# One large product a step ahead of the scores, the values of a pair in two runs, and norm rows on VectorE

## The chip, the core and the metric

The kernel runs on one core of a Trainium2 chip. The metric is the device time of one execution in microseconds (us). Engines are named as in the profile: PE is TensorE, DVE VectorE, ACT ScalarE, POOL GpSimd, SP SyncE, which issues the DMAs. Each engine takes its own instructions strictly one after the other, so an instruction that waits holds up everything behind it on its engine.

## The reference

One layer of a diffusion backbone with 128 context tokens and 1024 latent tokens, that is nine blocks of 128 tokens (block 0 is the context), of width 1024. Two head groups, attention and a bidirectional mLSTM, read one input projection and share one output projection, and a SwiGLU FFN follows. Cut to the part that the change touches:

```python
q = rope(rmsnorm(h @ w_q, q_norm_w))                  # 8 query heads of 64, 2 key/value heads
s = einsum('bqhgd,bkhd->bhgqk', q, k) * scale         # latent block: 128 rows x 1152 keys (1024 latent + 128 cached)
o = einsum('bhgqk,bkhd->bqhgd', softmax(s), v)
x = x + g1 * (concat([o, hm], -1) @ w_out)            # hm: the mLSTM heads; w_out has an hm half and an attention half
h2 = rmsnorm(x, norm2_w) * (1 + sc2) + sh2
x = x + g2 * swiglu(h2, w_gu, w_down)
```

Operands are split in a high and a low part (`hi`, `lo`), and three products stand for one, which keeps float32 accuracy.

## The kernel before

The program is written in three parts: projections and the mLSTM scan, then attention, then the FFN. The change is in the second. It is a loop over 64 heads (8 latent blocks of 8 query heads), one head a step, with an order that is written by hand (`manual_schedule`): each engine's instructions stand in the order in which the Python code emits them.

**What a step does for the softmax** (`step(n)`, L1490). PE makes the scores of head n+2 (`head_scores`, six matmuls into the PSUM tile `S`, L1110). `S` has five banks; even and odd heads lie at its two ends and share the middle bank. DVE forms the reciprocal of head n's sum (L1506), then the maximum of head n+1 (`head_max`, L1114), then the low part of head n's probabilities (`pl`, L1517). ACT makes the high part of head n (`ph`, L1509) and the exponential of head n+1 (`head_exp`, L1118). SP turns `ph` and `pl` by DMA. The scores of head n+2 take the place of head n's, so they wait for the exponential of head n. The maximum of head n+1 stands behind the scores of head n+2 in the program and reads the bank that they share with it.

**The values.** Two heads make a pair, and in each odd step PE multiplies the turned probabilities of an earlier pair with the values (`value_products`, L1053, 18 matmuls into `po`). ACT and POOL add up the result one step later (`value_sums`, L1058 to L1061).

**The fillers.** All other work of this part is cut into tasks (generators), and a planner (`Filler`, L1232) puts their pieces into the steps: the second half of the query projection (`q_task`), its rope, which runs on POOL, the turning of the queries (`turn_task`), the hm half of the output projection (`hm_task`), its attention half with the second norm (`mix_task`), and the splitting of `w_out` (`w_task`). Each piece names its engine, a cost and the least number of steps since the piece before it. Each engine has a credit a step, and a piece is taken while the credit is above zero and the piece's condition holds. `fl.run("PE")` emits the PE pieces; the ACT and DVE pieces of a step are emitted at its end, behind that step's `ph`, exponential and `pl`. A large piece on PE is half of a block's query projection or one `out_block` (L1138): 12 matmuls of 512 columns. Two PSUM banks serve all fillers. A product's bank is free again when DVE has read it (`add_gated`, L1133, which makes a tile `t` that POOL adds to `x`), a turned block's when DVE has made its low part (`ring`, `qT`).

**Rows of the second norm.** `norm_rows` (L1428) scales a block's 1024 columns by its reciprocal root mean square, in two ACT instructions of 512 columns (L1432); PE turns them, ACT and DVE apply the modulation.

## Time and profile before

| what | us |
|---|---|
| median of 3 runs (lowest, highest) | 1640.9 (1636.6, 1645.5) |
| the profiled execution's own time | 1645.3 |
| its span, first to last instruction | 1643.5 |
| PE, DVE, ACT, POOL busy | 1489.5, 902.0, 732.4, 251.1 |
| first maximum of the loop's filler steps to the last one (455.88 to 799.94 in the span) | 344.1 |
| from there to the first FFN product (837.45) | 37.5 |

The profiled execution is 4.4 us above the median. The page gives busy time and the costliest groups of instructions for the whole span; for the loop, the views over stretches and the instructions in order of time say more, since engines wait for each other there in every step.

### The profile page before, as it was taken

How to read it: one execution, taken by the hardware profiler on the slowest of the kernel's cores; microseconds unless marked ns; L12 is line 12 of the kernel's file. 1: busy time of each engine (PE TensorE's matmuls, PEld its weight loads, DVE VectorE, ACT ScalarE, POOL GpSimd, SP SyncE). 2: the span in 40 equal slices, each digit the busy share in tenths (PEclk: the TensorE clock that was granted, in tenths of full speed). 3: DMA queues.
4: the chain of work that ended last, by engine and by line, in shares of the span. 5: the costliest groups of instructions: out<-in, count | busy, mean ns of one | idle time of the engine just before them, and what ended most of it. 6: DMA issues, size and time to landing. Idle time of an engine off the chain costs nothing.

```text
span 1643.5 us, 22904 instructions
## 1 busy us (share of the span) xinstructions
PE 1489.5 (91%) x8651; PEld 921.1 (56%) x8651; DVE 902.0 (55%) x2160; ACT 732.4 (45%) x1428; POOL 251.1 (15%) x272
## 2 busy tenths in 40 slices
PE   5899999898596799877689989999999999999995
PEld 2755666575454677655455555456664466655542
DVE  3844355849765777877645456333353333442278
ACT  3744343345465666778655666003340032422023
POOL 0411021303224522333320000000000000000001
PEclk8899999999598899999799999999999999999998
DMA  9345462301285789556357553421104310120213
GB/s 353 114 142 150 93 144 62 73 1 19 60 174 99 149 190 193 101 102 127 72 180 252 184 194 100 140 93 52 52 27 141 115 52 28 50 77 14 83 59 116
DMA packets 281685, 181.83 MB, mean 111 GB/s; under 512 B 167302, under 2 KB 253782, under 8 KB 281574
## 3 DMA queue, kind: packets, MB, share of 16 engines
q1 hardware_dynamic: 280150, 177.96, 41.6%
q10 hardware_dynamic: 1424, 2.40, 0.4%
q8 instruction: 68, 1.11, 0.3%
q14 instruction: 43, 0.35, 0.1%
HBM read 122.71 MB, written 19.29 MB: 86 GB/s over the span
## 4 chain that ended last, share of the span: by engine, by line
PE 37%; DMA 5%; DVE 4%; ACT 4%; issue 1%; POOL 0%; ACTq 0%; SPq 0%; DVEq 0%; POOLq 0%
PE mm L1180 8%; PE mm L1182 8%; PE mm L1181 8%; PE mm L1751 4%; PE mm L1752 4%; PE mm L1753 4%; DMA wd_d<-wdt 3%; DMA wdt<-in_w_down_dram 2%; DVE x L1136 1%; ACT wdt L1546 1%; DVE wdt L1552 1%; ACT wdt L1551 1%; DVE t L1135 1%; ACT jk L1576 0%; ACT jk L1837 0%
## 5 line engine op out<-in xcount | busy, mean ns | idle before, releaser
L1180 PE MATMUL mm<-h,wpair 128*128 128x384 f16 x1056 | 345.0, 327 | 1.5 <-DVE fl L1453 1.5
L1181 PE MATMUL mm<-h,wpair 128*128 128x384 f16 x1056 | 345.0, 327 | 0.0
L1182 PE MATMUL mm<-h,wpair 128*128 128x384 f16 x1056 | 344.7, 327 | 0.0
L1714 DVE SCALAR_TENSOR_TENSOR tn<-tn,mm 128x384 f32<-128x384 f32 x66 | 36.4, 552 | 217.5 <-PE mm L1182 139.6
L1751 PE MATMUL mm<-wd,hl 128*128 128x512 f16 x396 | 149.9, 379 | 0.0
L1752 PE MATMUL mm<-wd,hl 128*128 128x512 f16 x396 | 149.9, 379 | 0.0
L1753 PE MATMUL mm<-wd,hl 128*128 128x512 f16 x396 | 149.6, 379 | 0.0
L1180 PEld LDWEIGHTS <-wpair 128*128 128x128 f16 x1056 | 105.4, 100 | 67.3 <-issue 0.7
L1182 PEld LDWEIGHTS <-wpair 128*128 128x128 f16 x1056 | 103.5, 98 | 68.7 <-issue 0.7
L1181 PEld LDWEIGHTS <-wpair 128*128 128x128 f16 x1056 | 103.5, 98 | 68.7 <-issue 2.3
L1110 PE MATMUL S<-kst,qT 128*128 128x512 f32 (+1 forms) x384 | 97.3, 394 | 47.9 <-ACT pr L1118 46.0
L499 PE MATMUL wi<-ipair,hT 128*128 128x384 f16 (+2 forms) x384 | 124.7, 325 | 2.8 <-ACT ipair L216 2.8
L1840 POOL TENSOR_TENSOR x<-x,fw 128x512 f32<-128x512 f32 x9 | 11.5, 1274 | 756.7 <-ACT jk L1837 756.7
L501 PE MATMUL wi<-ipair,hT 128*128 128x384 f16 (+2 forms) x384 | 124.4, 325 | 0.4 <-POOL hT L135 0.4
L500 PE MATMUL wi<-ipair,hT 128*128 128x384 f16 (+2 forms) x384 | 124.7, 325 | 0.0
L1717 ACT ACTIVATE jk<-tn 128x384 bf16<-128x384 f32 x66 | 34.4, 521 | 196.8 <-DVE tn L1715 145.1
L1576 ACT ACTIVATE jk<-braw 128x1024 bf16<-128x1024 f32 x44 | 45.9, 1044 | 152.9 <-DVE x L1136 152.1
L1517 DVE SCALAR_TENSOR_TENSOR pl<-pr,st,ph 128x1152 f16<-128x1152 f32 x64 | 95.1, 1486 | 31.9 <-ACT ph L1509 29.0
L1509 ACT ACTIVATE ph<-pr,st 128x1152 f16<-128x1152 f32 x64 | 80.3, 1254 | 68.0 <-issue 59.6
L1110 PEld LDWEIGHTS S<-kst,qT 128*128 128x128 f32 x384 | 69.9, 208 | 72.2 <-ACT pr L1118 58.6
L1114 DVE TENSOR_REDUCE st<-S 128x1 f32<-128x1152 f32 x64 | 86.7, 1355 | 39.9 <-PE S L1110 39.4
L1135 DVE SCALAR_TENSOR_TENSOR t<-mm,gm,gl 128x512 f32<-128x512 f32 x64 | 47.7, 745 | 81.3 <-PE mm L1753 81.3
(427 smaller groups left out, 2854.5 us busy)
## 6 DMA issues: line engine op xcount, KB each, us to landing
wd<-wd_d SPq DMA_DIRECT2D x58, 512.0 KB
braw<-in_w_gu_dram SPq DMA_DIRECT2D x44, 512.0 KB
a4s<-in_w_ada_dram SPq DMA_DIRECT2D x32, 512.0 KB
wdt<-in_w_down_dram SPq DMA_DIRECT2D x22, 512.0 KB
wd_d<-wdt SPq DMA_DIRECT2D x22, 512.0 KB
aw<-in_w_ada_dram SPq DMA_DIRECT2D x16, 512.0 KB
x<-in_x_sample_dram SPq DMA_DIRECT2D x16, 512.0 KB
iraw<-in_w_in_dram SPq DMA_DIRECT2D x32, 256.0 KB
```

The lines of the kernel that those rows point to most:

```text
L499: mm(ps[:, :n], ah, wh[:, k % 2, c0 : c0 + n], start=(k == 0), stop=False)
L500: mm(ps[:, :n], ah, wl[:, k % 2, c0 : c0 + n], start=False, stop=False)
L501: mm(ps[:, :n], al, wh[:, k % 2, c0 : c0 + n], start=False, stop=(k == KD - 1))
L1110: mm(S[:, lo:hi], qTs[b][:, h, :], kst[kv][:, t, lo:hi], start=(t == 0), stop=(t == 1))
L1114: dve.tensor_reduce(out=stat[n][:, 0:1], in_=score[n], axis=AX.X, op=ALU.max, negate=True)
L1180: mm(ps, wh[:, k, :], th[:, k, :], start=(k == 0), stop=False)
L1181: mm(ps, wh[:, k, :], tl[:, k, :], start=False, stop=False)
L1182: mm(ps, wl[:, k, :], th[:, k, :], start=False, stop=(k == KD - 1))
L1517: dve.scalar_tensor_tensor(out=pl, in0=pr, scalar=st[:, 3:4], in1=ph, op0=ALU.mult, op1=ALU.subtract)
L1751: mm(ps, ah, w[:, k, 0], start=(j + k == 0), stop=False)
L1752: mm(ps, ah, w[:, k, 1], start=False, stop=False)
L1753: mm(ps, al, w[:, k, 0], start=False, stop=(j + k == g["nf"] - 1))
```

## The change

- Within a step the order on PE is now: the second part of a pair's values (even steps), the fillers, the scores of head n+2, the first part of a pair's values (odd steps). Before, the scores came first, then the fillers, then a whole pair's values.
- The 18 value matmuls of a pair are issued as 10 at the end of an odd step and 8 at the start of the next; their sums are emitted in the step of the second part.
- The planner takes at most one PE piece of a cost over 2.0 in a step, and the credit of PE is 3.3 a step, before 3.5.
- The rope of a pair of query blocks starts no earlier than three steps after the previous pair's rope was emitted; before, it only had to be emitted.
- `norm_rows` is one DVE instruction of 1024 columns in place of two ACT instructions of 512, for the nine blocks, with one buffer; `norm2`, which does the last block, calls it too.
- The loop runs for at least one more step.

```diff
@@ -1042,12 +1042,13 @@
             return q_rest[:, b - CB].rearrange("p (k g) d -> p k (g d)", g=2)
         return ap2.tile([P, 4, P], F32, name=nm("oT"), tag="oT", bufs=3)
 
-    def value_products(b, j, nk, kv, rhs):
-        if j == 0:
+    def value_products(b, j, nk, kv, rhs, po=None, part=(0, NB)):
+        if j == 0 and po is None:
             oT[b] = new_oT(b)
-        po = po2[:, n_po[0] % 2 * 256 : n_po[0] % 2 * 256 + 256]
-        n_po[0] += 1
-        for n in range(nk):
+        if po is None:
+            po = po2[:, n_po[0] % 2 * 256 : n_po[0] % 2 * 256 + 256]
+            n_po[0] += 1
+        for n in range(nk)[slice(*part)]:
             v = vs[:, NB if nk == 1 else n, kv].rearrange("p t d -> p (t d)")
             for t in range(2):
                 mm(po, v, rhs(t, n), start=(n == 0 and t == 0), stop=(n == nk - 1 and t == 1))
@@ -1151,11 +1152,9 @@
         both = new() if new else fp.tile([P, KD, P], F32, name=nm("fl"), tag="fl", bufs=1)
         cnd = 0 if b == 0 else 1
         pss = []
-        for half in range(2):
-            y = fp.tile([P, 512], F32, name=nm("y"), tag="y", bufs=2)
-            act(y, x1[b][:, half * 512 : (half + 1) * 512], AF.Copy, scale=rs[b])
-            pss.append(y)
-            yield 0.1
+        pss += norm_rows(b)
+        yield 0.1
+        yield 0.1
         for half, y in enumerate(pss):
             ps = bank()
             for j in range(4):
@@ -1233,7 +1232,7 @@
 
         def __init__(self, **per_step):
             self.per_step, self.credit = per_step, dict.fromkeys(per_step, 0.0)
-            self.tasks, self.step, self.banks = [], 0, 2
+            self.tasks, self.step, self.banks, self.big = [], 0, 2, -1
 
         def add(self, gen):
             self.tasks.append([gen, None, self.step - 1])
@@ -1252,6 +1251,10 @@
                         break
                     if not behind and self.credit.get(engine, 1.0) <= 0.0 or ready is not None and not ready():
                         break
+                    if engine == "PE" and cost > 2.0:
+                        if self.big == self.step:
+                            break
+                        self.big = self.step
                     if engine in self.credit:
                         self.credit[engine] -= cost
                     self.banks -= need
@@ -1265,7 +1268,7 @@
         def free(self, n=1):
             self.banks += n
 
-    fl = Filler(PE=3.5, ACT=1.9, DVE=2.0)
+    fl = Filler(PE=3.3, ACT=1.9, DVE=2.0)
     at = {}
 
     def stamp(name):
@@ -1293,7 +1296,7 @@
         fl.free()
         if rope is None:
             return
-        yield "ACT", 1.1, 0, 0, lambda: b - 2 < CB or ("rope", b - 2) in at
+        yield "ACT", 1.1, 0, 0, lambda: b - 2 < CB or since(("rope", b - 2), 3)
         next(rope)
         yield "DVE", 1.1
         next(rope)
@@ -1398,7 +1401,7 @@
         rs[b] = rsqrt1(w, 1.0 / D)
         if b == NB - 1:
             return
-        yield "ACT", 1.35, 1, 0, lambda: b == 0 or ("turned", b - 1) in at
+        yield "DVE", 0.75, 1, 0, lambda: b == 0 or ("turned", b - 1) in at
         ys = norm_rows(b)
         yield "PE", 1.5, 1, 2
         pss = norm_turn(ys)
@@ -1426,12 +1429,9 @@
         return w
 
     def norm_rows(b):
-        ys = []
-        for half in range(2):
-            y = fp.tile([P, 512], F32, name=nm("y"), tag="y", bufs=2)
-            act(y, x1[b][:, half * 512 : (half + 1) * 512], AF.Copy, scale=rs[b])
-            ys.append(y)
-        return ys
+        y = fp.tile([P, D], F32, name=nm("y"), tag="y", bufs=1)
+        dve.tensor_scalar(out=y, in0=x1[b], scalar1=rs[b], scalar2=None, op0=ALU.mult)
+        return [y[:, 0:512], y[:, 512:1024]]
 
     def norm_turn(ys):
         pss = []
@@ -1491,16 +1491,20 @@
         b, h = heads[n] if n < len(heads) else (NB, 0)
         fl.step = n
         fl.begin()
-        if n + 2 < len(heads):
-            head_scores(n + 2)
-        fl.run("PE")
         now = []
         if n < 2:
             now = [value_products(*first_values[2 * n + i]) for i in range(2)]
-        elif n % 2 == 1 and (n - 3) // 2 in pairs:
+        elif n % 2 == 0 and half:
+            args, po = half.pop()
+            now = [value_products(*args, po, (5, NB))]
+        fl.run("PE")
+        if n + 2 < len(heads):
+            head_scores(n + 2)
+        if n % 2 == 1 and (n - 3) // 2 in pairs:
             m = (n - 3) // 2
             two = pairs.pop(m)
-            now = [value_products(heads[2 * m][0], m % 4, NB, m % 4 // 2, lambda t, i: two[t][:, :, i, :])]
+            args = (heads[2 * m][0], m % 4, NB, m % 4 // 2, lambda t, i: two[t][:, :, i, :])
+            half.append((args, value_products(*args, None, (0, 5))[2]))
         if n < len(heads):
             st, pr = stat.pop(n), prob.pop(n)
             dve.reciprocal(st[:, 2:3], st[:, 1:2])
@@ -1516,13 +1520,8 @@
                 head_exp(n + 1)
             dve.scalar_tensor_tensor(out=pl, in0=pr, scalar=st[:, 3:4], in1=ph, op0=ALU.mult, op1=ALU.subtract)
             dma_t(two_n[1][:, h % 2, :, :], pl)
-        for v in late:
+        for v in now:
             value_sums(*v)
-        late[:] = now
-        if n < 2:
-            for v in late:
-                value_sums(*v)
-            late[:] = []
         fl.run("X")
         for behind in (False, True):
             for e in ("ACT", "DVE"):
@@ -1606,7 +1605,7 @@
             dve.tensor_scalar(out=v[:, 7:8], in0=v[:, 4:5], scalar1=v[:, 5:6], scalar2=wds[:, self.f, 3:4], op0=ALU.mult, op1=ALU.mult)
 
 
-    pairs, late = {}, []
+    pairs, half = {}, []
     pieces = [Piece(0, lambda: wp.tile([P, 1024], F32, name=nm("braw"), tag="raw", bufs=2), ("whi", "wlo"))]
     pieces += [Piece(f) for f in range(1, NF)]
     with tc.manual_schedule(engines=ENGINES):
@@ -1632,7 +1631,7 @@
         head_max(0)
         head_exp(0)
         n = 0
-        while n < len(heads) + 4 or fl.tasks:
+        while n < len(heads) + 5 or fl.tasks:
             step(n)
             if n >= len(heads):
                 fl.credit = dict.fromkeys(fl.credit, 5.0)
```

How this moves instructions on PE, around the hm half of the output projection (`mm<-wlo,ring` is such a product, `S` the scores, `ident` marks a turning, and `[waits ...]` names the engines whose counters the instruction waits for). Before, between the scores of heads 29 and 31:

```order
L1110 MATMUL S_4796<-kst_4271,qT_5807 128x512 x4
L1142 MATMUL mm_6250<-wlo_5012,ring_5704 128x512 [waits DVE_49,PE_49]
...
L1144 MATMUL mm_6250<-wlo_5015,ring_5704 128x512
L1110 MATMUL S_4796<-kst_4271,qT_5807 128x512 [waits Activation_49]
L1110 MATMUL S_4796<-kst_4271,qT_5807 128x512 x3
L1110 MATMUL S_4796<-kst_4271,qT_5807 128x128 x2
```

And now, between the same scores:

```order
L1143 MATMUL mm_6219<-wlo_5199,ring_5761 128x512 [waits DVE_49]
...
L1111 MATMUL S_4796<-kst_4271,qT_5798 128x128 [waits Activation_49]
L1111 MATMUL S_4796<-kst_4271,qT_5798 128x128
L1111 MATMUL S_4796<-kst_4271,qT_5798 128x512 x4
L114 MATMUL mm_6260<-ident,t_1157_6120 128x128 [waits DMAHW7_49,DVE_49]
L114 MATMUL mm_6260<-ident,t_1157_6120 128x128 x3
L1143 MATMUL mm_6265<-wlo_4999,ring_5762 128x512 [waits DVE_49]
...
L1111 MATMUL S_4796<-kst_4271,qT_5798 128x512 [waits Activation_49]
```

In both lists scores and large products take turns. What moved is the product's step: before, the product that stands behind the scores of head 30 was emitted in step 28; now it is emitted in step 29, ahead of the scores of head 31. The DVE counter that it waits for is that of the row `t_1182` below, in step 28 on DVE, which reads the bank of the product before it (`mm_6219`):

```order
L1115 TENSOR_REDUCE st_6246<-S_4796 128x1 [waits PE_49]
L1521 SCALAR_TENSOR_TENSOR pl_6241<-pr_6201,st_6199,ph_6240 128x1152 [waits DMAHW2_49,Activation_49]
L1134 TENSOR_TENSOR t_1182_6257<-mm_6219,gl_4866 128x512 [waits Pool_49]
L1510 RECIPROCAL st_6246<-st_6246 128x1 [waits Activation_49]
```

The first of these rows is the maximum of head 29, and the PE counter that it waits for is reached by the scores of head 30, as before the change. So the row that frees the bank now stands on DVE behind a maximum that needs the scores just ahead of the product.

The second place is the first turning of query block 3 on PE, which reads what the rope on POOL has written (`q_rest`). Before, and then now:

```order
L1110 MATMUL S_4796<-kst_4270,qT_4856 128x512 [waits Activation_49]
L1110 MATMUL S_4796<-kst_4270,qT_4856 128x512 x3
L1110 MATMUL S_4796<-kst_4270,qT_4856 128x128 x2
L114 MATMUL mm_5342<-ident,q_rest 128x128 [waits DVE_49,PE_49,Pool_49]
L114 MATMUL mm_5342<-ident,q_rest 128x128 x3
L1287 MATMUL mm_5301<-ipair_4262,hT_293 128x512
```

```order
L1111 MATMUL S_4796<-kst_4270,qT_4856 128x512 x4
L114 MATMUL mm_5306<-ident,q_rest 128x128 [waits PE_49,Activation_49,Pool_49]
L114 MATMUL mm_5306<-ident,q_rest 128x128 x3
L1290 MATMUL mm_5268<-ipair_4262,hT_293 128x512
...
L1111 MATMUL S_4796<-kst_4270,qT_4856 128x512 [waits Activation_49]
```

The turning is in step 9 in both. Before, it stood behind the scores of head 11; now those scores stand behind it. The rope that it waits for was emitted in step 6 before and is emitted in step 7 now.

## The prediction

> **What bounds the kernel now.** I read the view by stretches first, cut at the maxima of heads 3, 21, 44 and 63 and at the first FFN product (columns: us, then busy us of PE, its weight loads, DVE, ACT and POOL, each with its instructions, PE's granted clock, DMA share, GB/s).
>
> ```profile
> 455.88:566.10 110.22, 86.33 (x448) 57.96 (x447) 74.49 (x124) 67.72 (x93) 49.02 (x44) 0.89 0.67 128
> 566.10:684.25 118.15, 108.99 (x601) 86.45 (x600) 95.29 (x137) 81.18 (x112) 36.26 (x44) 1.00 0.86 175
> 684.25:799.94 115.69, 88.29 (x471) 66.99 (x472) 88.27 (x172) 88.33 (x141) 43.55 (x46) 0.95 0.57 107
> 799.94:837.45 37.51, 24.65 (x105) 18.00 (x104) 14.97 (x42) 17.96 (x32) 13.59 (x15) 0.80 0.48 130
> 837.45:1643.50 806.05, 780.40 (x4418) 432.97 (x4417) 356.00 (x852) 270.04 (x517) 16.66 (x13) 0.99 0.31 98
> ```
>
> The FFN holds half of the span with PE busy for 97% of it, and no edit reaches into it but one norm. In the loop (the first three rows, 60 steps in 344 us, 5.7 us a step) PE is busy for 78, 92 and 76%, and no engine is full: what sets the step is who waits for whom. The view of waits over the same 344 us (in total, times, longest):
>
> ```profile
> PEld S L1110 <- ACT pr L1118: 53.6, 33, 8.8
> PE S L1110 <- ACT pr L1118: 41.6, 25, 8.3
> DVE st L1114 <- PE S L1110: 35.2, 32, 3.2
> ACT pr L1118 <- DVE st L1114: 22.6, 21, 3.2
> ```
>
> That is a ring: scores wait for an exponential, a maximum for scores, an exponential for a maximum. The instructions in order of time show one turn of it (start, us, engine; heads 29 to 31):
>
> ```profile
> 604.42 1.42 PE L1110 MATMUL S<-kst,qT 128*128 128x128 f32 x6 [0.86 <-ACT pr L1118]
> 606.05 0.47 PE L1142 MATMUL mm<-wlo,ring 128*128 128x512 f32 x1 [0.21 <-DVE qT L135]
> 606.32 1.36 DVE L1114 TENSOR_REDUCE st<-S 128x1 f32<-128x1152 f32 x1
> 606.36 0.40 PE L1143 MATMUL mm<-wlo,ring 128*128 128x512 f32 x1
> 606.59 0.40 PE L1144 MATMUL mm<-wlo,ring 128*128 128x512 f32 x1
> 607.66 1.42 DVE L1517 SCALAR_TENSOR_TENSOR pl<-pr,st,ph 128x1152 f16<-128x1152 f32 x1
> 607.72 1.23 ACT L1118 ACTIVATE pr<-S,st 128x1152 f32<-128x1152 f32 x1
> 609.00 0.68 DVE L135 TENSOR_TENSOR ring<-mm,ring 128x512 fp32r<-128x512 f32 x1
> 609.08 1.37 PE L1110 MATMUL S<-kst,qT 128*128 128x512 f32 x6
> 609.60 0.68 DVE L1133 TENSOR_TENSOR t<-mm,gl 128x512 f32<-128x512 f32 x1
> 610.48 1.36 DVE L1114 TENSOR_REDUCE st<-S 128x1 f32<-128x1152 f32 x1
> 616.67 0.27 PE L1053 MATMUL po<-phT,vs 128*128 128x256 f16 x1
> 616.78 0.27 PE L1053 MATMUL po<-plT,vs 128*128 128x256 f16 x1
> 617.68 1.40 PE L1110 MATMUL S<-kst,qT 128*128 128x128 f32 x6
> 619.12 1.36 DVE L1114 TENSOR_REDUCE st<-S 128x1 f32<-128x1152 f32 x1 [2.12 <-PE S L1110]
> ```
>
> From the maximum at 606.32 to the next at 610.48 are 4.16 us: maximum, exponential (607.72), scores (609.08). The last two rows show that a maximum ends its wait with the scores just made, which are those of the head after its own. Beside this ring, at no cost, PE makes a large product (606.05 to the scores at 609.08: 3.03 us) and DVE makes `pl` and reads the bank of a product (609.60).
>
> **The change part by part.** *Fillers ahead of the scores.* Between the scores of two heads there is one large product before and after. The lists of instructions show what differs: the product there now belongs to the later step, and its first matmul waits for the DVE row at the end of the step before it, mostly for one of the two PSUM banks, since a turned block holds the other. That row stands on DVE behind a maximum, and this maximum behind the scores that have just left PE. The ring becomes longer: scores, maximum, `pl`, the bank's reading, product, scores. By the rows above: maximum to `pl` 1.34 (606.32 to 607.66), `pl` to the next row 1.34 (to 609.00), reading 0.68, product 3.03, scores to the next maximum 1.40 (609.08 to 610.48), in all 7.8 us where the short ring needs 4.2. Other rows that come first on DVE, ACT or POOL are added, from these groups (busy us, mean ns) and from the first and last row of a reciprocal root on DVE:
>
> ```profile
> L1133 DVE TENSOR_TENSOR t<-mm,gl 128x512 f32<-128x512 f32 x32 | 21.9, 686 | 17.9 <-PE mm L1144 17.8
> L135 DVE TENSOR_TENSOR qT<-mm,qT 64x512 fp32r<-64x512 f32 x12 | 8.3, 689 | 0.3
> L135 DVE TENSOR_TENSOR wlo<-raw,wlo 128x1024 fp32r<-128x1024 f32 x4 | 4.7, 1219 | 0.0
> L135 POOL TENSOR_TENSOR kst<-oT,kst 128x512 fp32r<-128x512 f32 x5 | 6.4, 1277 | 4.3 <-ACT kst L1419 4.1
> L1432 ACT ACTIVATE y<-x,r 128x512 f32<-128x512 f32 x16 | 10.6, 710 | 2.3 <-DVE r L1196 2.3
> L340 DVE TENSOR_SCALAR x<-x,ry 128x1024 f32<-128x1024 f32 x9 | 6.4, 750 | 0.0
> ...
> 802.73 0.15 DVE L1189 TENSOR_SCALAR r<-r 128x1 f32<-128x1 f32 x1
> 804.78 0.21 DVE L1196 TENSOR_SCALAR r<-r 128x1 f32<-128x1 f32 x1
> ```
>
> I went through the new list step by step and noted for each PE piece whether its wait ends in the step just before. For the stretch of heads 21 to 44 (23 steps): 17 such products, 17 x 7.8 = 132.6; rows ahead of the one waited for, 7.6 (a second 0.7 us evacuation in three steps, `w_out` splits of 1.22 and query halves of 1.4 in three more); two steps in which only transpositions wait, 12.2; four steps by the short ring or by PE alone (value run 2.0, which is 18 matmuls 0.11 apart, product 3.0, scores 1.4), 19.4. Sum 171.8 for 118.2: **+53.6**. Heads 44 to 63 (19 steps): 9 x 7.8 = 70.2; 15.0 for what comes first (POOL's 1.28 for a mix block, in five steps, the reciprocal root of about 2.2 in two, and a modulation that waits for POOL in one); five transposition steps 36.3 (6.7 to 9.1 each); five others 27.0. Sum 148.5 for 115.7: **+32.8**. Heads 3 to 21 (18 steps): four serial steps 33.1, thirteen of 4.3 to 6.6 together 70.1, and the rope's step, below, 17.4. Sum 120.6 for 110.2: **+10.4**. If a product's 12 matmuls cost their spacing alone (0.23 from 606.36 to 606.59, 2.76) and nothing is lost in between, a serial step is 7.2 and the 30 of them give 18 back; that is the lower bound of the unit price.
>
> *The rope.* Before, ACT waits 7.83 us for POOL:
>
> ```profile
> 486.10 1.90 POOL L669 TENSOR_TENSOR q_rest<-q_rest,ry 128x1024 f32<-128x1024 f32 x1 [1.00 <-POOL oT L1061]
> 495.36 2.34 POOL L687 TENSOR_TENSOR q_rest<-q_rest,nr 128x1024 f32<-128x1024 f32 x1
> 497.73 1.06 ACT L663 ACTIVATE nr<-q_rest 128x1024 f32<-128x1024 f32 x1 [7.83 <-POOL q_rest L687]
> 501.18 2.39 PE L1110 MATMUL S<-kst,qT 128*128 128x512 f32 x6 [8.26 <-ACT pr L1118]
> ```
>
> The new condition removes this wait. But the rope takes POOL 11.6 us (486.10 to 497.70) and is now emitted a step later, and the turning that reads it stands ahead of the scores of head 11. So PE is held until POOL is done: 11.4 from the step's maximum, then turning 0.9, half a projection 3.7, scores 1.4, which is the 17.4 above. The stall goes from ACT to PE and grows by a few us.
>
> *One large product a step.* Before, the five steps with two products stretch their step and the next (heads 29 to 31 to 8.6 between scores, 609.08 to 617.68). This goes; the sums above hold it.
>
> *Norm rows.* Per block, 2 x 0.71 leave ACT and, by the nearest row (L340, same shape), 0.75 comes to DVE. ACT is at most the second longest in the new steps, so I count no gain; at most it is 9 x 1.42 = 12.8. In three steps the row stands ahead of a bank's reading and is in their 6.7; were all nine exposed, 6.8.
>
> *Values in two runs.* Nothing stands between the two parts on PE, and their sums keep their place: 0. If an emission gap opened between them, it would fall into PE's idle time.
>
> *The end.* One product and one transposition move behind the last head, the last pair's values come earlier: of 37.5 us I take 2 off (bounds 4 off, 5 on).
>
> *PE's clock.* The longer ring leaves PE idle for about 3.3 us in each serial step without values. What idling does, the trace shows:
>
> ```profile
> 548.50:552.00 3.50, 3.23 (x11) 2.84 (x12) 1.40 (x4) 2.82 (x6) 3.42 (x3) 0.51 0.62 117
> 548.77 2.40 PE L1110 MATMUL S<-kst,qT 128*128 128x512 f32 x6 [2.79 <-ACT pr L1118]
> 815.61 0.80 PE L1142 MATMUL mm<-wlo,kst 128*128 128x512 f32 x1 [4.67 <-DVE fl L1453]
> 820.47 0.63 PE L1144 MATMUL mm<-whi,kst 128*128 128x512 f32 x1
> ```
>
> After 2.79 idle the scores take 2.40 in place of 1.40 at a granted 0.51; after 4.67 a product takes 5.3 (815.61 to its last at 820.47, and 0.43 more), 2.3 above 3.03. About 16 gaps of 3.2 us and more are new: none cold is 0, all cold 16 x 2.4 = 38. I take 10: the price of the shorter gap, 1.0, for ten of them, since 3.3 us is nearer to 2.79 than to 4.67 and not every gap need go cold. The Trainium skill (TensorE: Matmul & The Clock Gate, "Part 1: The HAM clock gate") says that the clock halves after an idle window of about 3.4 us; by this rule only the six or so longest gaps would count, an estimate of 6 x 1.7 = 10. Here the trace differs: 2.79 us was enough at 548.77.
>
> Sum: 10.4 + 53.6 + 32.8 - 2 + 10 = 105. Against the profiled execution, 1645.3 + 105 = 1750; that execution lies 4.4 above the median, so **1746** for the median.
>
> **The rivals.** (1) *The products fill the wait for the exponential.* If the DVE rows they wait for are done when PE comes to them, the order is a gain: the rope's 7.8, and about 8 for three double steps (12.8 for two steps, where two average ones take 10.4). 1640.9 - 16 = 1625. For it: PE idles 41.6 us ahead of scores. Against it: the wait in the list points at a row of the step before, behind the maximum, 3.4 us after the scores end, not before them. It decides if fewer than about four steps are serial, at 3.6 each. (2) *Bank waits do not bind.* If a product meets a free bank, some 19 of 26 products in the last two stretches wait for nothing late, at 2.5 each (7.8 less 5.3, the mean of 4.2 and 6.4): 1746 - 48 = 1698. For it: there are two banks and one product a step. Against it: a turned block holds one of them for two steps. (3) *A cold PE.* All 16 gaps cold: 28 more than I took, 1774. For it: both gaps quoted above went cold, the shorter one at 2.79 us.
>
> **How the numbers follow.** The forecast has a chance of 0.56, a cold PE 0.22, unbinding banks 0.14; the last 0.08 is (1) and what lies between it and no change: 0.05 for a gain, 0.03 for none. About 8.2 us, 0.5%, is what a measurement tells from no change. So slower 0.92, same 0.03, faster 0.05. The range goes from (2) less 8, for a unit price nearer 7.2, to (3) with 11 for the end and the norm rows: 1690 to 1785. It leaves (1) out.
>
> **What would show it.** Right: large products (L1143 to L1145) of the loop wait for DVE `t`, `ring` or `fl`, some 60 us in all, where scores wait for ACT `pr` now; maxima 7.5 to 8 us apart for heads 29 to 33, where PE is about two thirds busy; one turning that waits some 10 us for POOL `q_rest`, and no such wait of ACT L663; the FFN unchanged at about 806. Wrong: maxima 4 to 6 us apart there, or scores that still wait for `pr`. Half clock in one stretch of the loop would speak for (3).

## The result, and the profile after

The changed kernel takes 1787.6 us (median of four runs, 1787.2 to 1793.4), the kernel before, measured beside it on the same chip, 1643.2: a ratio of 1.089, interval 1.085 to 1.094. The forecast was 1746 with a range from 1690 to 1785. Direction and place were right, and the time lies 2.6 us above the range.

The view by stretches of the changed kernel, cut at the same heads as in the prediction and with the first three heads ahead of them, and that first stretch of the kernel before (us, then busy us of PE, its weight loads, DVE, ACT and POOL, PE's granted clock, DMA share, GB/s):

```profile
440.30:465.59 25.29, 13.79 (x51) 7.49 (x51) 8.81 (x12) 10.19 (x15) 2.25 (x5) 0.73 0.42 100
465.59:590.45 124.86, 89.69 (x430) 57.83 (x428) 76.02 (x123) 66.89 (x91) 44.01 (x39) 0.84 0.55 107
590.45:776.55 186.10, 128.37 (x594) 100.97 (x595) 90.37 (x126) 80.13 (x110) 37.88 (x45) 0.87 0.53 114
776.55:939.08 162.53, 112.13 (x474) 84.51 (x473) 89.61 (x185) 81.73 (x130) 43.78 (x48) 0.74 0.42 78
939.08:981.02 41.94, 25.34 (x114) 18.79 (x113) 21.10 (x48) 17.96 (x31) 17.78 (x17) 0.86 0.42 113
981.02:1791.60 810.58, 785.77 (x4418) 434.89 (x4417) 356.86 (x853) 268.66 (x515) 16.66 (x13) 0.98 0.31 97
```
```profile
439.86:455.88 16.02, 11.51 (x39) 6.61 (x40) 8.82 (x13) 10.09 (x15) 1.84 (x5) 0.68 0.70 163
```

Of the 148.1 us between the two profiled executions, 129.4 lie in the loop from head 3 to head 63 (+14.6, +68.0, +46.8), 9.3 in the first three heads, 4.4 between head 63 and the FFN, 4.5 in the FFN and 0.4 ahead of it all. PE has more busy time in the stretch of heads 21 to 44 (128.4 us for 109.0) with seven matmuls fewer in its records: its clock fell from 1.00 to 0.87.

The view of waits over heads 3 to 63 of the changed kernel (us in total, times, longest):

```profile
DVE st L1115 <- PE S L1111: 208.2, 52, 12.9
ACT pr L1119 <- DVE st L1115: 185.2, 49, 12.6
...
PE mm L1143 <- DVE t L1134: 29.6, 11, 5.5
...
PE S L1111 <- ACT pr L1119: 17.8, 13, 2.8
```

Before, scores waited 41.6 us for the exponential and the maximum 35.2 for the scores. Now the maximum waits 208 us for scores, and what these stand behind is a product that waits for a row of DVE. Two turns of the ring, heads 30 to 32, in order of time (start, us; rows of the ring alone):

```profile
665.85 1.36 DVE L1115 TENSOR_REDUCE st<-S 128x1 f32<-128x1152 f32 x1 [3.95 <-PE S L1111]
667.13 1.41 DVE L1521 SCALAR_TENSOR_TENSOR pl<-pr,st,ph 128x1152 f16<-128x1152 f32 x1
668.45 0.69 DVE L1134 TENSOR_TENSOR t<-mm,gl 128x512 f32<-128x512 f32 x1
669.19 0.51 PE L1143 MATMUL mm<-wlo,ring 128*128 128x512 f32 x1 [1.40 <-DVE t L1134]
672.09 1.32 PE L1111 MATMUL S<-kst,qT 128*128 128x128 f32 x6
673.44 1.36 DVE L1115 TENSOR_REDUCE st<-S 128x1 f32<-128x1152 f32 x1 [4.05 <-PE S L1111]
676.04 0.68 DVE L135 TENSOR_TENSOR ring<-mm,ring 128x512 fp32r<-128x512 f32 x1
676.83 0.63 PE L114 MATMUL mm<-ident,t 128*128 128x128 f32 x4 [3.42 <-issue]
677.47 0.53 PE L1143 MATMUL mm<-wlo,ring 128*128 128x512 f32 x1
681.89 1.26 PE L1111 MATMUL S<-kst,qT 128*128 128x512 f32 x6
683.19 1.36 DVE L1115 TENSOR_REDUCE st<-S 128x1 f32<-128x1152 f32 x1 [5.61 <-PE S L1111]
```

The first turn (665.85 to 673.44, 7.59 us) is the ring of the prediction: maximum, `pl`, the reading of a bank, product, scores. The second takes 9.75 us. Its transpositions add 0.64 (676.83 to 677.47). PE had been idle for 3.42 ahead of them; they still run at full speed, but most of the product behind them does not (granted clock 0.61 from 677.47 to 681.89), so that it needs 4.42 in place of 2.90 (669.19 to 672.09).

### The profile page after: what moved, and what is told of

It reads as the page before. It is cut to its first block, busy times and chain, and to the rows that moved or that the text cites. A ratio compares the mean times of both kernels' runs of the same rounds, so it can differ in the third digit from the quotient of the medians.

```text
span 1791.6 us, 22874 instructions
## 1 busy us (share of the span) xinstructions
PE 1544.3 (86%) x8651; PEld 957.4 (53%) x8651; DVE 907.1 (51%) x2169; ACT 722.8 (40%) x1410; POOL 252.5 (14%) x272
## 5 line engine op out<-in xcount | busy, mean ns | idle before, releaser
L1119 ACT ACTIVATE pr<-S,st 128x1152 f32<-128x1152 f32 x64 | 78.1, 1220 | 198.1 <-DVE st L1115 198.0
L1111 PE MATMUL S<-kst,qT 128*128 128x512 f32 (+1 forms) x384 | 102.2, 410 | 19.7 <-ACT pr L1119 18.0
L1716 ACT ACTIVATE jk<-tn 128x384 bf16<-128x384 f32 x66 | 34.4, 521 | 206.3 <-DVE tn L1714 151.6
L1111 PEld LDWEIGHTS S<-kst,qT 128*128 128x128 f32 x384 | 78.0, 225 | 43.0 <-ACT pr L1119 25.0
```

What stands on the lines that cost most here:

```text
L1111: mm(S[:, lo:hi], qTs[b][:, h, :], kst[kv][:, t, lo:hi], start=(t == 0), stop=(t == 1))
```

## Experiments

All times below are medians, each with its ratio to the kernel before, which ran beside it on the same chip. The medians of the kernel before lie between 1641.4 and 1644.8 us there, so a difference of a few us between two rows can come from that. The table gives, from the traces, the time from maximum to maximum by stretch, then from head 63 to the first FFN product, and the FFN.

| run | us | ratio (95%) | heads 0–3 | 3–21 | 21–44 | 44–63 | to FFN | FFN |
|---|---|---|---|---|---|---|---|---|
| before | 1643.2 | 1 | 16.0 | 110.2 | 118.2 | 115.7 | 37.5 | 806.1 |
| changed | 1787.6 | 1.089 (1.085–1.094) | 25.3 | 124.9 | 186.1 | 162.5 | 41.9 | 810.6 |
| changed, scores first | 1632.2 | 0.994 (0.991–0.996) | 17.6 | 105.4 | 119.2 | 105.4 | 42.6 | 802.0 |
| before, order alone | 1785.2 | 1.088 (1.084–1.092) | 18.8 | 130.1 | 180.3 | 168.8 | 37.3 | 813.7 |
| changed, banks read first | 1739.7 | 1.060 (1.057–1.063) | 25.8 | 122.6 | 145.8 | 147.9 | 43.6 | 811.9 |
| changed, all rows first | 1656.0 | 1.007 (1.005–1.009) | 19.0 | 108.2 | 120.3 | 122.7 | 37.5 | 803.0 |
| changed, maximum written first | 1694.3 | 1.029 (1.027–1.031) | 22.0 | 118.8 | 130.6 | 132.6 | 43.3 | 809.8 |
| changed, 16 extra matmuls | 1778.1 | 1.083 (1.080–1.086) | 25.8 | 123.4 | 176.5 | 160.7 | 41.4 | 814.5 |
| changed, 28 and 12 extra | 1770.0 | 1.076 (1.074–1.078) | 25.3 | 127.4 | 170.2 | 156.0 | 46.8 | 809.5 |
| changed, first values late | 1780.1 | 1.083 (1.081–1.086) | 16.1 | 124.7 | 186.1 | 162.5 | 44.0 | 809.9 |
| scores first, two products | 1640.4 | 0.998 (0.997–1.000) | 17.7 | 105.2 | 116.5 | 113.4 | 37.4 | 809.0 |
| scores first, turning later | 1632.5 | 0.993 (0.991–0.995) | 18.1 | 95.4 | 119.2 | 105.5 | 45.0 | 811.9 |
| the same, scale early | 1635.1 | 0.995 (0.993–0.997) | 16.4 | 96.5 | 118.9 | 105.5 | 46.2 | 811.9 |
| scores first, maximum early | 1679.2 | 1.022 (1.020–1.023) | 13.5 | 112.4 | 130.1 | 117.6 | 52.9 | 810.3 |
| maximum written first, turning later | 1685.0 | 1.024 (1.022–1.026) | 20.9 | 111.4 | 132.4 | 133.9 | 40.6 | 803.9 |

### Is it the order alone?

In the changed kernel, scores go back to the head of the step; in the kernel before, only the order of the two calls is swapped.

```diff
 # changed kernel, scores first
+        if n + 2 < len(heads):
+            head_scores(n + 2)
         now = []
...
         fl.run("PE")
-        if n + 2 < len(heads):
-            head_scores(n + 2)
 # kernel before, order alone
-        if n + 2 < len(heads):
-            head_scores(n + 2)
         fl.run("PE")
+        if n + 2 < len(heads):
+            head_scores(n + 2)
```

> The changed kernel with one edit undone: scores of head n+2 go to PE first in a step again, ahead of values and fillers; one large product a step, the rope's condition, values in two runs and norm rows on VectorE stay. Theory (the order of fillers and scores alone makes the loss, by the ring scores, maximum, pl, bank's reading, product, scores): about 1630 us, range 1610 to 1650, maxima of heads 29 to 33 about 4 to 6 us apart, half clock in the loop back to some 35 us. Rival (the planner's rule, the rope's condition or the norm rows carry a good part of it): 1670 or more.

> The kernel before with one edit alone: fillers ahead of the scores, everything else as it was, two large products in a step still allowed. Theory (the order alone makes the loss): 1780 us, range 1755 to 1815. Rival (the order costs only together with one product a step or the other edits): 1650 to 1720.

Measured 1632.2 and 1785.2. Undoing the order takes away all of the loss, and the order alone makes all of it; the other edits together, with the scores first, are worth a gain of 0.6%. With the scores first, the waits over heads 3 to 63 are close to those of the kernel before again, and PE's busy time at half clock there is 34.4 us (some 35 expected):

```profile
DVE st L1115 <- PE S L1111: 42.0, 30, 10.1
...
PE S L1111 <- ACT pr L1119: 31.2, 24, 2.9
```

### Where is the ring closed?

Three runs keep PE's order of the changed kernel and cut the ring at one link each. The first puts only the rows ahead of the maximum that read the bank of a product just made:

```diff
+            fl.run("DVE", True)
             if n + 1 < len(heads):
                 head_max(n + 1)
                 head_exp(n + 1)
```

> The changed kernel, order of PE kept; only the VectorE rows that read the bank of a product just made (L1134 and their like) are put ahead of the next maximum instead of behind it. This cuts the ring where my reading has it: the product no longer waits for a row that stands behind the maximum. Theory: a step in the stretch of heads 21 to 44 falls from 8.1 to 5 to 6 us, no wait of a large product for VectorE t there above 1 us; about 1665 us, range 1640 to 1700. Rival (what holds the product is something else: the transfers, ScalarE, or PE's clock): above 1740.

Measured 1739.7: a third of the loss comes back (48 of 144 us), and both theories miss: the time lies above the range of the first and just under the 1740 of its rival, and the step of heads 21 to 44 falls from 8.1 to 6.3 us on average and not to 5 to 6. Its rows in order of time show what still holds the product:

```profile
602.40 1.41 DVE L1522 SCALAR_TENSOR_TENSOR pl<-pr,st,ph 128x1152 f16<-128x1152 f32 x1
603.72 0.68 DVE L135 TENSOR_TENSOR ring<-mm,ring 128x512 fp32r<-128x512 f32 x1
604.55 0.48 PE L1143 MATMUL mm<-wlo,ring 128*128 128x512 f32 x1 [1.65 <-DVE st L1510]
```

The product reads `ring`, the low half of a turned block, and the VectorE row that makes it (L135, done at 604.40) still stands behind `pl`. The view names as the releaser the reciprocal right behind that row, which the product does not read. So the second run moves all of the fillers' rows, on ScalarE and VectorE, and the values' sums:

```diff
+        for v in now:
+            value_sums(*v)
+        fl.run("X")
+        for behind in (False, True):
+            for e in ("ACT", "DVE"):
+                fl.run(e, behind)
+        # from here on as before: maximum, exponential, pl and its transposing DMA
         if n + 1 < len(heads):
             head_max(n + 1)
             head_exp(n + 1)
         dve.scalar_tensor_tensor(out=pl, ...)
         dma_t(...)
-        # values' sums and fillers' rows stood here
```

> The changed kernel, order of PE kept; now all rows that ScalarE and VectorE do for the fillers, and the sums of the values, stand ahead of the next maximum, its exponential and pl, not only the readings of a product's bank. In the run with those readings alone moved, steps of heads 22 to 25 still took 6.3 to 7.1 us because the product waited for the other half of the turned block (ring, L135), which still stood behind the maximum. Theory (the ring through the rows of VectorE): that wait goes too, steps there fall to 4.5 to 5.5 us, 1675 us, range 1650 to 1705. Rival (the rest is half clock and waits for ScalarE, POOL or transfers): no gain on the 1740 of the run with the readings alone, 1725 to 1760.

Measured 1656.0: 131.6 of the 144.4 us are back with PE's order unchanged, and in heads 21 to 44 a step takes 5.2 us. Of PE's waits over heads 3 to 63, the longest are now those for the exponential, as before the change. Products and transpositions wait for rows of VectorE three times, 2.6 us in all, where these waits come to 89 us in the changed kernel:

```profile
PE S L1111 <- ACT pr L1119: 32.6, 20, 3.8
...
PE mm L1143 <- DVE fl L1453: 1.0, 1, 1.0
PE mm L114 <- DVE fl L1453: 0.9, 1, 0.9
PE mm L1143 <- DVE t L1134: 0.7, 1, 0.7
```

This run moves ScalarE's rows and the sums along with VectorE's; what each of them brings was not taken apart.

The third run attacks the other link, from scores to maximum. Each head's maximum reads its own scores, made a step earlier, but it is written behind the scores of the next head, and the two heads lie in one PSUM tile, `S`, and share a bank of it. Written ahead of them, it becomes the one that they wait for:

```diff
         fl.run("PE")
+        if n < len(heads):
+            st, pr = stat.pop(n), prob.pop(n)
+            dve.reciprocal(st[:, 2:3], st[:, 1:2])
+            dve.tensor_scalar(out=st[:, 3:4], in0=st[:, 2:3], scalar1=2.0 ** 14, ...)
+        if n + 1 < len(heads):
+            head_max(n + 1)
         if n + 2 < len(heads):
             head_scores(n + 2)
...
-            st, pr = stat.pop(n), prob.pop(n)
-            dve.reciprocal(st[:, 2:3], st[:, 1:2])
-            dve.tensor_scalar(out=st[:, 3:4], in0=st[:, 2:3], scalar1=2.0 ** 14, ...)
...
-                head_max(n + 1)
                 head_exp(n + 1)
```

> The changed kernel with the maximum of head n+1 (and the two small rows ahead of it) written ahead of the scores of head n+2 instead of behind them. Each engine keeps its order; what changes is that the maximum no longer counts as a reader that comes after these scores, whose tile has a PSUM bank in common with its own; now these scores wait for the maximum. Theory (the first link of the ring is this shared bank: the maximum of a head waits for the scores of the next one, which it does not read): the ring is cut, VectorE reads the products' banks while PE makes scores, and PE's waits for VectorE's rows go; 1650 us, range 1620 to 1675. Rival (the maximum is late for its own scores or behind VectorE's other rows, and the shared bank costs nothing): above 1740.

Measured 1694.3: 93 of the 144 us come back by this dependence alone, less than the theory's 1650 (at most 1675). Its waits show what is left. The maximum's wait for scores is no longer in the list, and the exponential, which reads the same tile and is still written behind the scores, has taken its place:

```profile
ACT pr L1119 <- PE S L1111: 101.6, 50, 12.3
...
PE S L1111 <- DVE st L1115: 27.8, 16, 3.7
```

With the turning of a rope's block later in addition:

> As the run with the maximum written first, and the turning of a rope's block four steps after the rope instead of two. Theory (the rope's stall of about 10 us between heads 3 and 21 goes; a part of it comes back behind the loop, as in the run with the scores first, where 10.0 became nothing): 2 to 10 us under the run with the maximum first, and if that one is at 1640 or below, the fastest of all. Rival (the stall is hidden there): the same time.

Measured 1685.0, 9.3 less (10 expected at most). The stretch of heads 3 to 21 falls by 7.5.

### What does half clock cost?

Extra matmuls behind the scores keep PE busy where it would idle. They read constants and write the half of the values' bank that is free; their result is not used.

```diff
         if n + 2 < len(heads):
             head_scores(n + 2)
+        if 3 <= n < len(heads):   # first run: even n from 4 on, reps = 16
+            extra = po2[:, n_po[0] % 2 * 256 : n_po[0] % 2 * 256 + 256]
+            v = vs[:, 0].rearrange("p k t d -> p (k t d)")
+            reps = 12 if n % 2 else 28
+            for i in range(reps):
+                mm(extra, v[:, 0:P], v, start=(i == 0), stop=(i == reps - 1))
```

> The changed kernel with 16 extra matmuls of 128 rows by 256 on PE behind the scores of each even step from the fourth on (constant operands, into the free half of the values' bank, the result is not used), about 1.8 us each time. They are put where PE idles some 3.4 us and then starts at half clock. Theory (half clock costs about 30 us of the 144): 1757 us, range 1740 to 1775, PE's busy time at half clock in the loop falls from 137 us to under 90. Rival (half clock is hidden behind the waits): 1785 to 1800, no gain.

> The changed kernel with more extra matmuls than the run that had 16 in even steps: 28 behind the scores of each even step and 12 of each odd step (in odd steps the value run stands behind them), some 3.1 and 1.3 us. In the first run PE's busy time at half clock in the loop went from 137 to 76 us and the loop from 473.5 to 460.6. Theory (half clock costs the changed kernel about 25 to 40 us in the loop): busy time at half clock under 40 us, loop 440 to 452, 1765 us, range 1750 to 1775. Rival (the 12.8 was all there is, and the rest of half clock is hidden): 1775 to 1795.

Measured 1778.1 and 1770.0. From the trace's clock, PE's busy time at half clock between heads 3 and 63 is 28.9 us before, 136.6 in the changed kernel, 76.3 with 16 extra matmuls and 27.0 with 28 and 12. The loop (heads 3 to 63) goes from 473.5 to 460.6 and 453.7 us. The stretches of the last run:

```profile
465.55:592.96 127.41, 113.43 (x777) 85.12 (x776) 75.47 (x122) 66.61 (x91) 41.78 (x40) 0.96 0.55 105
592.96:763.15 170.19, 158.53 (x1049) 130.24 (x1047) 90.38 (x126) 79.57 (x110) 37.23 (x45) 0.99 0.59 125
763.15:919.20 156.05, 132.21 (x845) 106.29 (x845) 89.89 (x185) 82.10 (x131) 45.43 (x48) 0.94 0.44 81
```

The first run falls between its two theories, the second is in the range of the one that gives half clock a price; its loop is 1.7 us longer than the upper end expected. So the half clock that the change adds costs the loop at least 20 us, if the extra matmuls help by the clock alone. They cost time too (heads 3 to 21 take 2.5 us more with them), so the price is higher. From above it is bounded by what PE itself loses: taking each pair of adjacent matmuls at half clock against the median spacing of the same pair at full clock, an estimate of some 62 us in the changed kernel and 12 before, about 50 more.

### The first values, the planner's rule, the rope

Two small parts of the change were undone apart. In the first, the values of block 0 stand behind the scores of steps 0 and 1 again:

```diff
-        if n < 2:
-            now = [value_products(*first_values[2 * n + i]) for i in range(2)]
-        elif n % 2 == 0 and half:
+        if n >= 2 and n % 2 == 0 and half:
...
             head_scores(n + 2)
+        if n < 2:
+            now = [value_products(*first_values[2 * n + i]) for i in range(2)]
```

> The changed kernel with one piece moved back: in steps 0 and 1 the values of block 0's four pairs stand behind the scores again, not ahead of them. From the maximum of head 0 to that of head 3 it takes 25.3 us in the changed kernel and 16.0 before; the kernel before with the order of fillers alone takes 18.8. Theory (the 6.5 between them are these values, which wait for their transposing DMA and for the sums on ScalarE while the scores wait behind them): the stretch falls to about 19 us and the time to 1781, range 1776 to 1785. Rival (the fillers make this stretch long too): 24 to 26 us, time unchanged.

Measured 1780.1, and 16.1 us from head 0 to head 3, as before the change: all 9.2 of that stretch are these values (7.5 by the medians). In the changed kernel, they wait ahead of the scores for their transposing DMA and for the sums of the pair before:

```profile
444.86 0.37 PE L1054 MATMUL po<-phT,vs 128*128 128x256 f16 x1 [5.32 <-DMA phT<-ph]
446.63 2.48 PE L1111 MATMUL S<-kst,qT 128*128 128x128 f32 x6
454.92 0.37 PE L1054 MATMUL po<-phT,vs 128*128 128x256 f16 x1 [5.80 <-ACT ol L1060]
```

In the second, the kernel with the scores first loses the rule of one large product a step, and PE's credit is 3.5 again:

```diff
-                    if engine == "PE" and cost > 2.0:
-                        if self.big == self.step:
-                            break
-                        self.big = self.step
...
-    fl = Filler(PE=3.3, ACT=1.9, DVE=2.0)
+    fl = Filler(PE=3.5, ACT=1.9, DVE=2.0)
```

> The changed kernel with the scores first again (the run of 1632 us) and, in addition, without the rule of one large product a step (credit 3.5 again, two allowed). Theory of the prediction (steps with two products cost some 8 us more): 1640 us. Rival (the planner's rule is worth nothing, since the product only moves to another step): 1629 to 1635.

Measured 1640.4 against 1632.2 with the rule. So rule and credit together are worth the 8 us by the time, but the two traces do not show them where I had put them: heads 21 to 44 take 2.7 us more with it, heads 44 to 63 take 8.0 less, and from head 63 to the FFN 5.1 are given back, which is nothing in sum. The two profiled executions differ in the FFN (802.0 to 809.0) and ahead of head 0, which the rule does not touch. Where the 8 us come from stays open. What this run still has of the change (the rope's condition, the values in two runs, the norm rows) is worth 0.2%, interval 0.0 to 0.3.

Third, the turning that reads the rope's block is allowed four steps after the rope instead of two, with the scores first:

```diff
-        yield "PE", 0.7, 1, 1, lambda: (b < CB or since(("rope", b), 2)) and fl.step >= 8 * (b - 2) + 1
+        yield "PE", 0.7, 1, 1, lambda: (b < CB or since(("rope", b), 4)) and fl.step >= 8 * (b - 2) + 1
```

> The changed kernel with the scores first again (1632 us) and the turning of a rope's block allowed four steps after the rope instead of two. In the run with the scores first, PE still waits 6.9 us there for POOL's q_rest, at half clock behind it, and the step takes 16.3 us for a usual 5.5. Theory (the rope's stall is now PE's, because the turning stands ahead of the scores): it goes, 1623 us, range 1618 to 1628. Rival (the half projection waits for the same rope, or the rope is only late somewhere else): 1630 to 1635.

The stall goes: heads 3 to 21 take 95.4 us for 105.4. The time does not: 1632.5 for 1632.2. In the profiled executions, the FFN takes 811.9 us where it took 802.0, and the way to it 2.4 more. The waits of the FFN, first with the scores first and then with the later turning in addition, show where:

```profile
ACT wdt L1545 <- DMA wdt<-in_w_down_dram: 29.2, 14, 4.0
PE mm L1580 <- ACT jk L1575: 3.5, 3, 1.7
```
```profile
ACT wdt L1545 <- DMA wdt<-in_w_down_dram: 37.8, 15, 4.2
PE mm L1580 <- ACT jk L1575: 10.0, 4, 3.7
```

ScalarE waits longer for weights of the FFN, and PE behind it 6.5 us longer for the squares that it makes of the next piece. That the FFN's weights set this pace was not tested, and the two executions lie 3.2 below and 2.6 above the medians of their kernels, so a part of the difference is spread.

### Two attempts at the short ring

Both start from the kernel with the scores first. One takes the maximum of head n+2 a step earlier, behind `pl` of head n; the other (with the later turning) puts reciprocal and scale of head n+1 ahead of the fillers' rows.

```diff
 # maximum early
-                head_max(n + 1)
                 head_exp(n + 1)
             dve.scalar_tensor_tensor(out=pl, ...)
             dma_t(...)
+        if n + 2 < len(heads):
+            head_max(n + 2)
 # scale early
-            dve.reciprocal(st[:, 2:3], st[:, 1:2])
-            dve.tensor_scalar(out=st[:, 3:4], ...)
...
             dma_t(...)
+            if n + 1 < len(heads):
+                head_scale(n + 1)     # the same two rows, for the next head
```

> The changed kernel with the scores first again (the run of 1632 us), and the maximum of head n+2 as the last row of pl's group in step n instead of that of head n+1 ahead of pl in step n+1. So the maximum stands behind its own scores and ahead of those of the next head, and the ring falls from scores, maximum, exponential to scores, maximum or scores, exponential, 2.8 us. Theory (this ring is what binds the kernel before): PE becomes the bound in the stretch of heads 21 to 44, 110 to 114 us for 119; 1608 us, range 1595 to 1622. Rival (the maximum then holds up pl and the rows behind it on VectorE, or the fillers bind): 1628 or more.

> As the run with the turning four steps after the rope, and in addition the reciprocal and the scale of head n+1 (two VectorE rows of 0.16 us) stand right behind pl of head n, ahead of VectorE's rows for the fillers, instead of at the start of the next step. In the run with the scores first ScalarE's ph waits 57.6 us in 29 places with no releaser shown; these two rows stand just ahead of it behind the fillers' rows. Theory (ph and so the next exponential wait for the scale): 1612 us, range 1600 to 1621. Rival (VectorE then waits for the exponential ahead of the fillers' rows and gives the time back): 1622 or more.

Both were misses: 1679.2 and 1635.1, in both cases the time of the rival. With the maximum early, a new ring takes the place of the old. Its rows:

```profile
603.99 1.76 PE L1111 MATMUL S<-kst,qT 128*128 128x128 f32 x6 [2.14 <-DVE st L1115]
605.56 1.42 DVE L1520 SCALAR_TENSOR_TENSOR pl<-pr,st,ph 128x1152 f16<-128x1152 f32 x1 [1.37 <-ACT ph L1513]
607.13 1.36 DVE L1115 TENSOR_REDUCE st<-S 128x1 f32<-128x1152 f32 x1
608.54 2.40 PE L1111 MATMUL S<-kst,qT 128*128 128x512 f32 x6 [1.06 <-DVE st L1115]
```

The maximum stands behind `pl`, `pl` waits for `ph`, and the scores wait for the maximum of the head before, in the tile that they share: 4.55 us from scores to scores without any large product between them. The early scale changes nothing that can be told from the run beside it.

## Why the prediction was right and wrong

The mechanism was right and is shown: the order alone makes the loss, the ring runs through the rows at the end of the step (cut there, 131.6 of 144.4 us come back) and starts at the maximum that waits for the next head's scores (cut there, 93). Rival 1, a gain, falls with the order alone, and rival 2, free banks, with the 89 us for which PE waits for VectorE's rows. The signs named ahead came in the main: the large products wait 63 us for rows of DVE (some 60 forecast), the maxima of heads 29 to 33 lie 7.50, 7.59, 9.75 and 7.59 us apart (7.5 to 8 forecast), and ACT's wait for the rope is gone. Sum forecast +105, measured +148 between the profiled executions and +144 between medians.

**Fillers ahead of the scores: right in size.** The unit of 7.8 us measured 7.59 in the turn quoted above. With PE kept at 0.99 of its clock, the stretch of heads 21 to 44 took 170.2 us, where the sum without clock said 171.8. One link was named too narrowly: with the readings of the banks alone out of the way, only 48 us came back, and a product then waited for the other half of a turned block. The lower unit price of 7.2 does not follow from its rows: 7.8 with 2.76 for the product in place of 3.03 is 7.5, and 30 steps then give 8 back, not 18. The ring starts at the scores tile that two heads share. The Trainium skill (PSUM — Partial Sum Buffer, "PSUM bank collisions raise a hardware error") says that the compiler's scheduler makes any two instructions of different engines depend on each other if they touch the same bank and quadrant of partitions, reads and writes alike. This case fits that: moved in the text alone, the maximum's wait of 208 us left the list, and the exponential took one of 102. But the two heads lie in one tile as well, and no run tells whether the bank or the tile makes the dependence.

**PE's clock: the step that failed.** The sum took 10 for it, between none cold (0) and all cold (38). The runs put it between 20, in the loop alone, and about 50. The count of gaps was right: between heads 3 and 63, PE has 20 gaps of 3.2 us and more in the changed kernel and 3 before, 17 new ones for the 16 forecast. What failed is the step from there to ten cold gaps at 1.0 us each. 19 of the 20 were followed by half clock (less than the full clock granted in the next 3 us), and so were 13 of the 14 gaps between 2.0 and 3.2 us, which the forecast left out (5 of 6 before). In all, half clock came 29 times between heads 3 and 63 for 8 before, and the 21 more at 20 to 50 us cost 1.0 to 2.4 each. Here is a step that the sum had at 7.8 and 2.2 for a reciprocal root:

```profile
830.01 1.36 DVE L1115 TENSOR_REDUCE st<-S 128x1 f32<-128x1152 f32 x1 [5.17 <-PE S L1111]
832.61 0.15 DVE L1188 TENSOR_SCALAR r<-r 128x1 f32<-128x1 f32 x1
834.78 0.68 DVE L1134 TENSOR_TENSOR t<-mm,gl 128x512 f32<-128x512 f32 x1
835.51 0.80 PE L1143 MATMUL mm<-wlo,kst 128*128 128x512 f32 x1 [5.55 <-DVE t L1134]
840.80 1.63 PE L1111 MATMUL S<-kst,qT 128*128 128x512 f32 x6
842.46 1.36 DVE L1115 TENSOR_REDUCE st<-S 128x1 f32<-128x1152 f32 x1 [6.75 <-PE S L1111]
```

It takes 12.45 us: the root 2.2, the product 5.3 (835.51 to the scores at 840.80) in place of 2.9, the scores 1.66 (to the maximum at 842.46) in place of 1.35, and the ring's other rows. The product alone loses the 2.4 that the prediction had for its worst gaps. So rival 3, a cold PE, came together with the forecast, and its 38 lies within the bounds. In heads 3 to 63 the forecast was 22.6 us short of the measured 129.4, its 10 for the clock included. With 28 and 12 extra matmuls, heads 21 to 44 are down to the sum's value, while heads 44 to 63 are still at 156.0 for 148.5 and heads 3 to 21 at 127.4 for 120.6. How much of that is left-over half clock (18.7 of the 27.0 us are in heads 44 to 63), how much the extra matmuls, and how much a miscounted step, stays open. The Trainium skill (TensorE: Matmul & The Clock Gate, "HAM oscillation — how this bites in real kernels") takes half of the time at half clock as lost. By this rule the 107.7 us that the change adds would cost an estimate of 54; the runs here leave room for 20 to 50.

**A move that I priced at nothing.** The split of the values was not run alone; with the rope's condition and the norm rows it is worth 0.2% with the scores first. But in steps 0 and 1 the change also puts values ahead of scores, and there PE waits for a transposing DMA and for sums. This is 9.2 us in the trace of the run that moves them back, and it was missing from the sum.

**The rope: right.** Scores of the step came 16.1 us apart (506.04 to 522.10), for 17.4 forecast:

```profile
515.39 2.34 POOL L687 TENSOR_TENSOR q_rest<-q_rest,nr 128x1024 f32<-128x1024 f32 x1
517.78 1.12 PE L114 MATMUL mm<-ident,q_rest 128*128 128x128 f32 x4 [10.26 <-POOL q_rest L687]
522.10 1.45 PE L1111 MATMUL S<-kst,qT 128*128 128x512 f32 x6
```

Not foreseen was a transposition three steps earlier that waits 4.69 us for a DMA and holds the scores behind it; in heads 3 to 21, the forecast has +10.4 and the trace +14.6:

```profile
487.43 1.09 PE L114 MATMUL mm<-ident,t 128*128 128x128 f32 x4 [4.69 <-DMA t<-hm_d]
```

**One large product, norm rows.** The rule and the credit give the 8 us of rival 1 by the time; the traces do not place them in the steps that I named. That the norm rows gain nothing was not run alone; the 0.2% with the scores first holds them too.

**The end and the FFN: small misses.** From head 63 to the FFN the change costs 4.4, where I took 2 off within bounds of 4 off to 5 on. The FFN's 4.5 lie within what it differs between runs that leave it untouched (802 to 814).

So the range missed by its upper end, built from a cold PE of 38 at most and nothing for the first values. With the measured 9.2 for these and 20 for the clock, the same sum ends at 1645.3 + 10.4 + 53.6 + 32.8 - 2 + 9.2 + 20 - 4.4 = 1765, with 50 at 1795. The measured 1787.6 lies between.

## What to carry to other kernels

Ahead of a change in the order of PE, follow one full cycle through all in-order queues, and ask of each wait whether it is in the same step or one later: with the order alone changed, every product, bank and row was the same as before, and 8.8% came from products that waited for a row standing behind a wait for the scores just ahead of the product, half clock behind these waits included. If such a ring leaves PE idle for about 3 us in every step, add the half clock behind each gap to the price, through everything that PE does until it is fast again. And if the order is wanted, move the rows that release the products ahead of the row that waits (1656 us); the fastest version here was the change without the new order (1632 us, 0.6% under the kernel before, interval 0.4 to 0.9; with the later turning the same), and of 10 us more that were saved in the loop, none was left at the end.

## What the runs showed of the hardware

Needless work on PE made a kernel faster. With 28 and 12 extra matmuls in a step, the changed kernel took 1770.0 us for 1787.6, with 158.5 us of busy PE for 128.4 in the stretch of heads 21 to 44.

The length of a gap alone does not decide on the clock, though gaps of 2 us and more mostly brought half clock here (32 of 34 in heads 3 to 63 of the changed kernel). One product stayed at full speed behind 3.47 us (granted clock 1.00 from 741.07 to 744.00), another went to half clock behind 2.19 (0.50 from 899.89 to 903.00):

```profile
741.07 0.47 PE L1143 MATMUL mm<-wlo,ring 128*128 128x512 f32 x1 [3.47 <-DVE ring L135]
899.89 0.79 PE L1145 MATMUL mm<-whi,kst 128*128 128x512 f32 x1 [2.19 <-POOL kst L135]
```
